# Two-layer diffusion backbone on one core: layer norms that work in PSUM, high-part products first, MLP blocks three ahead

## The chip, the core and the metric

The kernel runs on one core of one Trainium2 chip. The metric is the time of one execution in microseconds (us) of device time, as the median of several runs. Five engines matter here: TensorE (PE in the profile, PEld for its weight loads), VectorE (DVE), ScalarE (ACT), GpSimd (POOL) and SyncE (SP), which issues most DMAs.

## What is computed

384 tokens (128 context, 256 latent; three tiles of 128) pass through two layers. The part of a layer around the change, from the reference:

```python
y, extra = mixer_fn(x * (1 + sc1) + sh1)
x = _layernorm(ALPHA * x + g1 * y, lp['ln1_g'], lp['ln1_b'])
h = x * (1 + sc2) + sh2
f = jnp.square(jax.nn.relu(h @ lp['w_up'])) @ lp['w_down']
x = _layernorm(ALPHA * x + g2 * f, lp['ln2_g'], lp['ln2_b'])
```

`mixer_fn` ends in a product with `w_o` (1024 x 1024). The MLP is 1024 to 4096 to 1024. The layer's output, modulated by the next layer's shift and scale, goes into the next input projection, whose first chunk has 416 columns.

## The kernel before

**Arithmetic.** Every float32 product is three float32r products of high and low parts (`mm3`, lines 119 to 122): high by high, then the two mixed ones. A part is made by a cast (ACT, line 281 for weights, 1207 for activations) and a subtraction (DVE, `split_low`, line 125). Weights come through a ring of four split tiles.

**PSUM.** There are eight banks of 512 columns: psa 3, pso 1, psg 2, psm 2. A product with `w_o` or `w_down` accumulates 3 token tiles x 2 halves of 512 columns in the six banks of psa, pso and psg; psm holds transposes and the MLP's up blocks.

**`out_product` (line 1233)** runs `w_o` (8 weight rows of 128) and `w_down` (32). All but the last four rows go over all six banks. The last four (REST) are then done token tile by token tile (`last_part`), so that the norm of tile 0 runs beside the matmuls of tile 1. From there to the end of the function everything is recorded under `in_order`: each compute engine keeps the order in which the code is written. I call this stretch a tail. There are four: after `w_o` and after the MLP in each layer, at about 370, 645, 1006 and 1281 us.

**A tail, per tile (`layer_norm`, line 1152).** `raw` takes a half from its bank (DVE: gate times bank into z, line 1164; plus ALPHA x, line 1165; statistics, line 1167). `stats` ends the mean and variance (DVE lines 1170 to 1173, POOL's power at line 188, POOL line 1174). `normalise` scales z (ACT line 1182; DVE line 1179 for the second half of tile 2). `turn` transposes z into two psm banks (PE line 1193), modulates from the bank into an SBUF tile `hx` in eight 128-column pieces (ACT line 1199; DVE line 1202 for the second half of tile 2) and casts both halves to the high part hTh (line 1207). `low` subtracts for hTl (line 125). `update` makes the new x on POOL (lines 1215, 1216).

**The product behind a norm** is `first_up` (384 columns of `w_up`, the MLP blocks 0 to 2, token-major) behind `w_o`, and `first_chunk` (416 columns) behind the first layer's MLP. Both use `mm3` for one row of weights after another, so the third matmul already needs hTl:

```python
following(0, 0, 1)
turn[1]()
low[1]()
following(0, 1, KT)
normalise[2]()
following(1, 0, 2)
turn[2]()
```

After `first_up`, `square_u` and `turn_u` (lines 1336 to 1350) square the blocks and transpose them back.

**The MLP** (`step_mlp`, line 1394) records the up block k + AHEAD and then the down product of block k; AHEAD is 2. Block f needs three of the eleven T1 buffers (r, uh, ul). Here a scheduler, not `in_order`, sets the engines' order.

**The last tail** has no product behind it. DVE ends the second half of tile 1 and both halves of tile 2 by itself (`end`, lines 1225 and 1227), POOL ends the rest, and the result is stored in halves (line 1418).

Of the kernel before, what the change touches and what calls it, by code (L numbers as in the profile page):

```python
# [9 lines left out]
F32 = mybir.dt.float32  # L10
# [6 lines left out]
P = 128  # L17
# [17 lines left out]
AHEAD = 2  # L35
# [58 lines left out]
def kernel(ctx, tc, a):  # L94
# [360 lines left out]
    for l in range(L):  # L455
# [696 lines left out]
        def layer_norm(t, banks, xt, consts, mod, final):  # L1152

            cnd = 0 if t == 0 else 1
            gb, lg_, lb_ = consts[cnd], consts[2], consts[3]
            st = p2.tile([P, 2, 6], F32, tag="lnst", name=nm("lnst"), bufs=2)
# [4 lines left out]
            lows = []  # L1161

            def raw(h):
                nc.vector.tensor_tensor(out=z[h], in0=banks[h], in1=gb[:, halves[h]], op=ALU.mult)  # L1164
                nc.vector.scalar_tensor_tensor(out=z[h], in0=xt[:, halves[h]], scalar=ALPHA, in1=z[h], op0=ALU.mult,  # L1165
                                               op1=ALU.add)
                nc.vector.bn_stats(st[:, h], z[h])  # L1167

            def stats():
                nc.vector.bn_aggr(mv, st)  # L1170
                nc.vector.tensor_scalar(out=rs[:, 0:1], in0=mv[:, 1:2], scalar1=EPS, scalar2=None, op0=ALU.add)  # L1171
                rsqrt(rs[:, 1:2], rs[:, 0:1], 1)
                nc.vector.tensor_scalar(out=rs[:, 2:3], in0=mv[:, 0:1], scalar1=-1.0, scalar2=None, op0=ALU.mult)  # L1173
                nc.gpsimd.tensor_tensor(out=rs[:, 3:4], in0=rs[:, 2:3], in1=rs[:, 1:2], op=ALU.mult)

            def normalise(n=2):
                for h in range(n):
                    if t == 2 and h == 1:
                        nc.vector.tensor_scalar(out=z[h], in0=z[h], scalar1=mv[:, 0:1], scalar2=rs[:, 1:2],
                                                op0=ALU.subtract, op1=ALU.mult)  # L1180
                    else:
                        nc.scalar.activation(z[h], z[h], AF.Identity, bias=rs[:, 3:4], scale=rs[:, 1:2])

            def turn():
                ms, mb = mod
                hxs = []
                lows.clear()
                for h in range(2):
                    tb = bank(psm)
                    hx = v2("hx")  # L1190
                    hxs.append(hx)
                    for i in range(4):
                        nc.tensor.transpose(tb[:, i * P:(i + 1) * P], z[h][:, i * P:(i + 1) * P], ident)
                    for i in range(4):
                        k = 4 * h + i
                        o = hx[:, i * P:(i + 1) * P]
                        src = tb[:, i * P:(i + 1) * P]
                        if t < 2 or h == 0:
                            nc.scalar.activation(o, src, AF.Identity, bias=mb[:, k, cnd:cnd + 1],
                                                 scale=ms[:, k, cnd:cnd + 1])  # L1200
                        else:
                            nc.vector.tensor_scalar(out=o, in0=src, scalar1=ms[:, k, cnd:cnd + 1],
                                                    scalar2=mb[:, k, cnd:cnd + 1], op0=ALU.mult, op1=ALU.add)
                for h in range(2):
                    hv = hxs[h].rearrange("p (k n) -> p k n", k=4)
                    dh, dl = (q[:, 4 * h:4 * h + 4, t * P:(t + 1) * P] for q in hT)
                    nc.scalar.copy(dh, hv)
                    lows.append((dl, hv, dh))

            def low():  # L1210
                for q in lows:
                    split_low(*q)

            def update(h):
                nc.gpsimd.tensor_tensor(out=xt[:, halves[h]], in0=z[h], in1=lg_[:, halves[h]], op=ALU.mult)
                nc.gpsimd.tensor_tensor(out=xt[:, halves[h]], in0=xt[:, halves[h]], in1=lb_[:, halves[h]], op=ALU.add)
# [5 lines left out]
            def end(n):  # L1222

                for h in range(2 - n, 2):
                    nc.vector.scalar_tensor_tensor(out=z[h], in0=z[h], scalar=mv[:, 0:1], in1=lg_[:, halves[h]],  # L1225
                                                   op0=ALU.subtract, op1=ALU.mult)
                    nc.vector.scalar_tensor_tensor(out=xt[:, halves[h]], in0=z[h], scalar=rs[:, 1:2],  # L1227
                                                   in1=lb_[:, halves[h]], op0=ALU.mult, op1=ALU.add)
                    final(t, xt, halves[h])

            return raw, stats, normalise, turn, low, update, end

        def out_product(n_k, lhs, rhs, norm, rest, following, step=None, between=lambda i: None):
# [17 lines left out]
            raw, stats, normalise, turn, low, update, end = zip(*lns)  # L1251

            def last_part(t, within=None):
                steps = [(h, i) for h in range(2) for i in range(rest)]
# [5 lines left out]
                for n, (h, i) in enumerate(steps):  # L1260
                    if within and n == 2:
                        within()
                    w, x = tail[i]
                    mm3(banks[2 * t + h], tuple(q[:, t * P:(t + 1) * P] for q in x),
                        tuple(q[:, h * 512:(h + 1) * 512] for q in w), False, i == rest - 1)
                for h in range(2):
                    raw[t](h)
                    if within and h == 0:
                        low[t - 2]()
                stats[t]()  # L1270

            with in_order():
                last_part(0)
                normalise[0]()
                update[0](0)
                last_part(1)
                if following is None:
                    update[0](1)
                    end[1](1)
                    normalise[1](1)  # L1280
                    update[1](0)
                    last_part(2)
                    end[2](2)
                    return
                update[0](1)
                last_part(2, turn[0])
                normalise[1]()
                following(0, 0, 1)
# [6 lines left out]
                low[2]()  # L1295
                update[1](0)
                update[1](1)
                following(1, 2, KT)
                update[2](0)
                update[2](1)  # L1300
                between(0)
                following(2, 0, 3)
                stream.ahead(1)
                between(1)
                following(2, 3, KT)
                between(2)
                stream.ahead()
                between(3)
# [44 lines left out]
        def first_evac(i):  # L1353
            if i == 0:
                square_u(0)
            elif i == 1:
                square_u(1)
                turn_u(0)
            elif i == 2:
                turn_u(1)  # L1360
            else:
                square_u(2)
                turn_u(2)
# [3 lines left out]
        def first_up(t, k0, k1):  # L1367
            if k0 == 0:
                u_banks.append(bank(psa))
            proj_part(u_banks[t], w_u0, U0 * P, t, k0, k1)  # L1370
# [23 lines left out]
        def step_mlp(k):  # L1394
# [27 lines left out]
        def first_chunk(t, k0, k1):  # L1422
            if k0 == 0:
                banks_a.append(bank(psa))
            proj_part(banks_a[t], w_next, A_W, t, k0, k1)
# [163 lines left out]
```

## Time and profile before

| | us |
|---|---|
| median of 3 runs | 1311.73 |
| lowest, highest | 1308.55, 1313.06 |
| the profiled execution | 1311.86 |
| its span, first to last instruction | 1310.1 |
| PE busy in the span | 1273.6 (97%) |
| DVE, ACT, POOL busy | 882.9, 572.7, 207.2 |
| mean granted TensorE clock | 0.993 |

The profile comes from one execution; 1.8 us of that execution lie outside its span. PE's matmuls are pipelined: a row's duration is longer than the distance to the next one's start, so a loss is read from starts, or from the idle time that a row names in brackets together with what ended it.

### The profile page before, as it was taken

To read this page: it belongs to the slowest core of one execution; us is meant where nothing else is said; L and a number is where in the kernel's file an instruction comes from. 1 tells how busy PE (TensorE), PEld (TensorE's weight loads), DVE (VectorE), ACT (ScalarE), POOL (GpSimd) and SP (SyncE) were. 2 spreads that over 40 slices of the span, in tenths; PEclk is the share of its full clock that TensorE was granted. 3 is DMA by queue.
4 is the path that set the end of the run, shared out by engine and by line. 5 is a ranking of instruction groups with operands and counts; after the bars stand their busy time and mean duration, and the time that the engine had idled before them with its cause. 6 is when DMAs were issued, how large, how long until landed. Compare 5 with 4: busy or idle time off the path is not lost. (4 is left out here: it accounts for less than half of the span.)

```text
span 1310.1 us, 19402 instructions
## 1 busy us (share of the span) xinstructions
PE 1273.6 (97%) x7350; PEld 1143.7 (87%) x7350; DVE 882.9 (67%) x1603; ACT 572.7 (44%) x1054; POOL 207.2 (16%) x218
## 2 busy tenths in 40 slices
PE   8899999999999999999999999999999899999996
PEld 5789888999987999999988988899998799999995
DVE  4555899996669999543484689967455893333336
ACT  4454345323534444454365545423343644444441
POOL 0010301323223000000071120012320600000003
PEclk9999999999999999999999999999999999999998
DMA  9832354666534888554313224553644263335321
GB/s 368 295 109 91 103 173 158 210 217 222 163 112 163 274 272 271 177 171 140 113 72 121 86 93 161 182 173 118 227 159 153 72 225 129 129 129 183 133 71 49
DMA packets 64686, 211.68 MB, mean 162 GB/s; under 512 B 9233, under 2 KB 13265, under 8 KB 64465
## 3 DMA queue, kind: packets, MB, share of 16 engines
q1 hardware_dynamic: 61872, 201.49, 45.6%
q0 software_dynamic: 2432, 8.42, 1.9%
q8 instruction: 58, 0.95, 0.3%
q10 hardware_dynamic: 288, 0.52, 0.1%
q14 instruction: 36, 0.29, 0.1%
HBM read 206.28 MB, written 4.13 MB: 161 GB/s over the span
## 5 line engine op out<-in xcount | busy, mean ns | idle before, releaser
L125 DVE TENSOR_TENSOR wl<-raw,wh 128x1024 fp32r<-128x1024 f32 x250 | 317.5, 1274 | 284.9 <-ACT wh L281 281.2
L281 ACT CAST wh<-raw 128x1024 fp32r<-128x1024 f32 x250 | 261.7, 1050 | 453.3 <-PE bank L121 300.0
L120 PE MATMUL bank<-hTh,wh 128*128 128x384 f32 x976 | 330.8, 339 | 0.0
L122 PE MATMUL bank<-hTh,wl 128*128 128x384 f32 x976 | 328.1, 336 | 0.0
L121 PE MATMUL bank<-hTl,wh 128*128 128x384 f32 x976 | 328.0, 336 | 0.0
L120 PEld LDWEIGHTS bank<-hTh,wh 128*128 128x128 f32 x976 | 183.8, 188 | 6.7 <-issue 2.2
L121 PEld LDWEIGHTS bank<-hTl,wh 128*128 128x128 f32 x976 | 183.7, 188 | 2.4 <-issue 0.3
L122 PEld LDWEIGHTS bank<-hTh,wl 128*128 128x128 f32 x976 | 183.7, 188 | 0.6 <-issue 0.3
L121 PE MATMUL bank<-wl,uh 128*128 128x512 f32 x384 | 150.4, 392 | 0.0
L122 PE MATMUL bank<-wh,ul 128*128 128x512 f32 x384 | 150.2, 392 | 0.0
L120 PE MATMUL bank<-wh,uh 128*128 128x512 f32 x384 | 149.4, 391 | 0.0
L370 DVE CUSTOM_DVE_ANT_0 acc<-raw,csr,bT 128x1024 bf16<-128x1024 f32 x80 | 103.7, 1319 | 0.0
L120 PE MATMUL bank<-wh,hTh 128*128 128x256 f32 x336 | 100.6, 299 | 2.8 <-ACT tmc L594 2.8
L1107 POOL TENSOR_TENSOR tt<-tt,tt 128x384 f32<-128x384 f32 x48 | 61.6, 1304 | 242.3 <-DVE tt L1106 235.7
L370 DVE CUSTOM_DVE_ANT_0 acc<-lnc,csr,bT 128x1024 bf16<-128x1024 f32 x80 | 99.6, 1278 | 0.0
L121 PE MATMUL bank<-wl,hTh 128*128 128x256 f32 x336 | 96.0, 286 | 0.0
L122 PE MATMUL bank<-wh,hTl 128*128 128x256 f32 x336 | 95.9, 285 | 0.0
L120 PEld LDWEIGHTS bank<-wh,uh 128*128 128x128 f32 x384 | 72.0, 188 | 15.4 <-ACT wh L281 0.8
L122 PEld LDWEIGHTS bank<-wh,ul 128*128 128x128 f32 x384 | 72.0, 188 | 15.0
L121 PEld LDWEIGHTS bank<-wl,uh 128*128 128x128 f32 x384 | 72.1, 188 | 13.8
L120 PEld LDWEIGHTS bank<-wh,hTh 128*128 128x128 f32 x336 | 64.7, 193 | 6.8 <-ACT tmc L594 3.1
L121 PEld LDWEIGHTS bank<-wl,hTh 128*128 128x128 f32 x336 | 64.8, 193 | 2.5 <-issue 1.6
(260 smaller groups left out, 1862.3 us busy)
## 6 DMA issues: line engine op xcount, KB each, us to landing
raw<-in_w_g_dram SPq DMA_DIRECT2D x64, 512.0 KB, 3.6
raw<-in_w_d_dram SPq DMA_DIRECT2D x64, 512.0 KB, 3.5
raw<-in_w_u_dram SPq DMA_DIRECT2D x58, 512.0 KB, 3.7
raw<-in_w_av_dram SPq DMA_DIRECT2D x40, 512.0 KB, 3.4
lnc<-in_w_av_dram SPq DMA_DIRECT2D x40, 512.0 KB, 4.4
raw<-in_w_q_dram SPq DMA_DIRECT2D x28, 512.0 KB, 4.5
raw<-in_w_ada_dram SPq DMA_DIRECT2D x16, 512.0 KB, 8.5
raw<-in_w_b_dram SPq DMA_DIRECT2D x16, 512.0 KB, 3.6
```

The lines of the kernel that those rows point to most:

```text
L120: mm(out, lhsT=a_hl[0], rhs=b_hl[0], start=start, stop=False)
L121: mm(out, lhsT=a_hl[0], rhs=b_hl[1], start=False, stop=False)
L122: mm(out, lhsT=a_hl[1], rhs=b_hl[0], start=False, stop=stop)
L125: nc.vector.tensor_tensor(out=low, in0=x, in1=high.bitcast(F32), op=ALU.subtract)
L281: nc.scalar.copy(wh, raw)
L370: nc.vector.tensor_tensor_reduce(out=alloc().bitcast(BF16), in0=w, in1=csr[:, c], scale=1.0, scalar=bT[:, l, u, b:b + 1], op0=ALU.mult, op ...
L1107: nc.gpsimd.tensor_tensor(out=acc[c], in0=acc[c], in1=t_, op=ALU.add)
```

## The change

- `raw` multiplies in the bank in place and reads it from there for the sum. In the first three tails z is still an SBUF tile; in the last one everything stays in the banks.
- `turn` modulates in the psm bank in place, for all three tiles the first half on ACT and the second on DVE; the tile `hx` is gone. The cast (`high`) and the subtraction (`low`) read the bank.
- `proj_high` does both products of hTh first (16 matmuls), `proj_low` the eight of hTl last.
- The order within a tail is rewritten: transposes of tile 0 after one step of tile 2's matmuls rather than two, POOL's update of tile 0 after the statistics of tile 1.
- AHEAD is 3, and the third transposition of the squared blocks moves behind the first up block.
- The last tail computes the last half of tile 2 in two pieces of 256 columns; tile 1 is ended by ACT and POOL, with one last addition on DVE.

```diff
-AHEAD = 2
+AHEAD = 3
+        def proj_high(b, w, n, t, k0, k1):
+            for k in range(k0, k1):
+                for i in range(2):
+                    mm(b[:, :n], lhsT=hcol(k, t)[0], rhs=w[k][i], start=k == 0 and i == 0, stop=False)
+        def proj_low(b, w, n, t):
+            for k in range(KT):
+                mm(b[:, :n], lhsT=hcol(k, t)[1], rhs=w[k][0], start=False, stop=k == KT - 1)
...
+            src = banks if mod is None else z
...
-                nc.vector.tensor_tensor(out=z[h], in0=banks[h], in1=gb[:, halves[h]], op=ALU.mult)
-                nc.vector.scalar_tensor_tensor(out=z[h], in0=xt[:, halves[h]], scalar=ALPHA, in1=z[h], op0=ALU.mult,
-                                               op1=ALU.add)
-                nc.vector.bn_stats(st[:, h], z[h])
+                nc.vector.tensor_tensor(out=banks[h][:, c], in0=banks[h][:, c], in1=gb[:, c0:c1], op=ALU.mult)
+                nc.vector.scalar_tensor_tensor(out=src[h][:, c], in0=xt[:, c0:c1], scalar=ALPHA, in1=banks[h][:, c],
+                                               op0=ALU.mult, op1=ALU.add)
+                for i in range(c.start, c.stop, width):
+                    nc.vector.bn_stats(st[:, len(groups)], src[h][:, i:i + width])
...
-                        o = hx[:, i * P:(i + 1) * P]
-                        src = tb[:, i * P:(i + 1) * P]
-                        if t < 2 or h == 0:
-                            nc.scalar.activation(o, src, AF.Identity, bias=mb[:, k, cnd:cnd + 1],
+                        o = tb[:, i * P:(i + 1) * P]
+                        if h == 0:
+                            nc.scalar.activation(o, o, AF.Identity, bias=mb[:, k, cnd:cnd + 1],
...
+                            nc.vector.tensor_scalar(out=o, in0=o, scalar1=ms[:, k, cnd:cnd + 1],
...
+                def first_turn():
+                    turn[0]()
+                    high[0](0)
+                    normalise[1]()
+                    high[0](1)
+                    update[0](0)
+                    update[0](1)
+                last_part(2, first_turn)
+                sums(2, lambda: (low[0](0), low[0](1)))
+                following(0, 0, 4)
                 turn[1]()
-                low[1]()
-                following(0, 1, KT)
+                high[1](0)
                 normalise[2]()
-                following(1, 0, 2)
+                high[1](1)
+                low[1](0)
+                low[1](1)
+                following(0, 4, KT)
+                following(0)
+                following(1, 0, 4)
                 turn[2]()
...
+                    normalise[1]()
+                    update[1](0, 0)
+                    cuts = (0, 512, 768, 1024)
+                    last_part(2, None, cuts)
+                    sums(2, None, cuts)
+                    for h in range(2):
+                        for part in range(2):
+                            end[2](h, part)
+                    update[1](1, 0)
+                    update[1](0, 1)
+                    update[1](1, 1, nc.vector)
...
+            if k == 0:
+                with held(last_issued()):
+                    turn_u(2)
```

How this moves instructions, at three places. First DVE in the first layer's `w_o` tail, from the second half of tile 2 (z_4037, bank_3886) to tile 2's first low part. hTl is the low part, hx_4180 and hx_4190 are the modulated halves of tile 1. Before:

```order
L1164 TENSOR_TENSOR z_4037<-bank_3886,lnc_3857 128x512
L1165 SCALAR_TENSOR_TENSOR z_4037<-x_3873,z_4037 128x512
L1167 BN_STATS lnst_4033<-z_4037 128x6
L1170 BN_AGGR lnmv_4034<-lnst_4033 128x2
L1171 TENSOR_SCALAR lnrs_4035<-lnmv_4034 128x1
L1173 TENSOR_SCALAR lnrs_4035<-lnmv_4034 128x1
L125 TENSOR_TENSOR hTl<-hx_4180,hTh 128x4x128
L125 TENSOR_TENSOR hTl<-hx_4190,hTh 128x4x128
L1179 TENSOR_SCALAR z_4037<-z_4037,lnmv_4034,lnrs_4035 128x512
L1202 TENSOR_SCALAR hx_4244<-bank_4243,ms_3863,mb_3865 128x128 x4
L125 TENSOR_TENSOR hTl<-hx_4234,hTh 128x4x128
```

And now, where bank_4182 and bank_4191 hold tile 1's modulated halves:

```order
L1178 TENSOR_TENSOR bank_3886<-bank_3886,lnc_3857 128x512
L1179 SCALAR_TENSOR_TENSOR z_4037<-x_3873,bank_3886 128x512
L1182 BN_STATS lnst_4033<-z_4037 128x6
L1186 BN_AGGR lnmv_4034<-lnst_4033 128x2
L1187 TENSOR_SCALAR lnrs_4035<-lnmv_4034 128x1
L1191 TENSOR_SCALAR lnrs_4035<-lnmv_4034 128x1
L1216 TENSOR_SCALAR bank_4191<-bank_4191,ms_3863,mb_3865 128x128 x4
L1197 TENSOR_SCALAR z_4037<-z_4037,lnmv_4034,lnrs_4035 128x512
L125 TENSOR_TENSOR hTl<-bank_4182,hTh 128x4x128
L125 TENSOR_TENSOR hTl<-bank_4191,hTh 128x4x128
L1216 TENSOR_SCALAR bank_4240<-bank_4240,ms_3863,mb_3865 128x128 x4
L125 TENSOR_TENSOR hTl<-bank_4231,hTh 128x4x128
```

The low parts of tile 1 moved behind the scaling of tile 2's second half, four modulations were added ahead of it, and the operands named hx became banks.

Second PE at the same tail, around the transposes of tile 2 (ident, z_4036 and z_4037), with the product of tile 1 in bank_4226 before and bank_4222 now (o_ tiles are the parts of `w_up`). Before:

```order
L121 MATMUL bank_4226<-o_3914,hTh 128x384
L122 MATMUL bank_4226<-o_3913,hTl 128x384
L1193 MATMUL bank_4233<-ident,z_4036 128x128 x4
L1193 MATMUL bank_4243<-ident,z_4037 128x128 x4
L120 MATMUL bank_4226<-o_3937,hTh 128x384
L121 MATMUL bank_4226<-o_3938,hTh 128x384
L122 MATMUL bank_4226<-o_3937,hTl 128x384
```

And now:

```order
L607 MATMUL bank_4222<-o_3937,hTh 128x384
L607 MATMUL bank_4222<-o_3938,hTh 128x384
L1208 MATMUL bank_4231<-ident,z_4036 128x128 x4
L1208 MATMUL bank_4240<-ident,z_4037 128x128 x4
L607 MATMUL bank_4222<-o_3973,hTh 128x384
L607 MATMUL bank_4222<-o_3974,hTh 128x384
```

No product of hTl stands ahead of the transposes any more; the eight of them follow at the end of the tile's product.

Third POOL in the last tail, from the power of tile 1 (lnrs_12402 before, lnrs_12384 now; x_10058 and x_10046 are tile 0, x_10060 and x_10048 tile 1). Before:

```order
L188 TENSOR_TENSOR lnrs_12402<-lnrs_12402,nhalf 128x1
L1174 TENSOR_TENSOR lnrs_12402<-lnrs_12402 128x1
L1215 TENSOR_TENSOR x_10058<-z_12399,lnc_12245 128x512
L1216 TENSOR_TENSOR x_10058<-x_10058,lnc_12247 128x512
L1215 TENSOR_TENSOR x_10060<-z_12403,lnc_12245 128x512
L1216 TENSOR_TENSOR x_10060<-x_10060,lnc_12247 128x512
L188 TENSOR_TENSOR lnrs_12407<-lnrs_12407,nhalf 128x1
```

And now:

```order
L188 TENSOR_TENSOR lnrs_12384<-lnrs_12384,nhalf 128x1
L1192 TENSOR_TENSOR lnrs_12384<-lnrs_12384 128x1
L1233 TENSOR_TENSOR x_10046<-z_12380,lnc_12265 128x512
L1236 TENSOR_TENSOR x_10046<-x_10046,lnc_12267 128x512
L1233 TENSOR_TENSOR x_10048<-z_12385,lnc_12265 128x512
L188 TENSOR_TENSOR lnrs_12389<-lnrs_12389,nhalf 128x1
L1233 TENSOR_TENSOR x_10048<-z_12386,lnc_12265 128x512
L1236 TENSOR_TENSOR x_10048<-x_10048,lnc_12267 128x512
```

Two POOL passes over tile 1 now follow the power of tile 2, which stood last before.

## Rows read from the trace of the kernel before

**Rows 1.** The page: busy time of each engine over the span.
```profile
PE 1273.6 (97%) x7350; PEld 1143.7 (87%) x7350; DVE 882.9 (67%) x1603; ACT 572.7 (44%) x1054; POOL 207.2 (16%) x218
```
**Rows 2.** Waits of PE: total us, times, longest us, over the whole span.
```profile
PE bank L1193 <- DVE z L1179: 5.0, 3, 1.7
PE bank L122 <- DVE hTl L125: 3.9, 5, 1.0
...
PE bank L1345 <- DVE r L1339: 1.7, 2, 0.8
```
**Rows 3.** Timeline of PE, layer 0 `w_o` tail: start, us, operation, idle before.
```profile
382.60 1.03 PE L1193 MATMUL bank<-ident,z 128*128 128x128 f32 x8
...
387.58 0.33 PE L120 MATMUL bank<-o,hTh 128*128 128x384 f32 x1
387.75 0.34 PE L121 MATMUL bank<-o,hTh 128*128 128x384 f32 x1
389.08 0.45 PE L122 MATMUL bank<-o,hTl 128*128 128x384 f32 x1 [0.98 <-DVE hTl L125]
...
394.87 0.44 PE L122 MATMUL bank<-o,hTl 128*128 128x384 f32 x1 [0.47 <-DVE hTl L125]
...
397.96 0.66 PE L1193 MATMUL bank<-ident,z 128*128 128x128 f32 x4 [1.69 <-DVE z L1179]
```
**Rows 4.** Timeline of DVE, the same tail.
```profile
391.72 0.21 DVE L1170 BATCH_NORM_AGGREGATE lnmv<-lnst 128x2 f32<-128x12 f32 x1
...
393.51 2.99 DVE L125 TENSOR_TENSOR hTl<-hx,hTh 128x512 fp32r<-128x512 f32 x2 [1.33 <-ACT hTh L1207]
396.43 1.48 DVE L1179 TENSOR_SCALAR z<-z,lnmv,lnrs 128x512 f32<-128x512 f32 x1
398.73 1.37 DVE L1202 TENSOR_SCALAR hx<-bank,ms,mb 128x128 f32<-128x128 f32 x4 [0.82 <-PE bank L1193]
```
**Rows 5.** Timeline of POOL, the same tail.
```profile
394.35 1.61 POOL L1216 TENSOR_TENSOR x<-x,lnc 128x512 f32<-128x512 f32 x1
395.92 1.71 POOL L1215 TENSOR_TENSOR x<-z,lnc 128x512 f32<-128x512 f32 x1
```
**Rows 6.** Timeline of ACT, the same tail: z of tile 0.
```profile
380.73 1.52 ACT L1182 ACTIVATE z<-z,lnrs 128x512 f32<-128x512 f32 x2 [9.12 <-POOL lnrs L1174]
```
**Rows 7.** Single lines 1164 and 1165: duration ns min/median/max, first and last start.
```profile
L1164 DVE TENSOR_TENSOR z<-bank,lnc x24: 673/686/692, 374.6 to 1300.2; 128x512 f32<-128x512 f32 x24
L1165 DVE SCALAR_TENSOR_TENSOR z<-x,z x24: 691/693/1544, 375.4 to 1300.9; 128x512 f32<-128x512 f32 x24
```
**Rows 8.** Groups by line and form: busy us, mean ns, idle before.
```profile
L125 DVE TENSOR_TENSOR o<-bank,o 128x384 fp32r<-128x384 f32 x12 | 6.6, 552 | 4.0 <-ACT o L681 3.8
L633 DVE TENSOR_TENSOR bank<-bank,cst 128x128 f32<-128x128 f32 x16 | 4.5, 291 | 1.5 <-PE bank L626 1.5
L125 DVE TENSOR_TENSOR hTl<-hx,hTh 128x384 fp32r<-128x384 f32 x8 | 4.4, 555 | 1.7 <-ACT hTh L496 1.7
L125 DVE TENSOR_TENSOR ul<-bank,uh 128x128 fp32r<-128x128 f32 x18 | 4.1, 280 | 1.8 <-ACT uh L1348 1.8
L949 DVE TENSOR_TENSOR atts<-bank,dtab 128x256 f32<-128x256 f32 x16 | 6.0, 413 | 0.0
...
L1199 ACT ACTIVATE hx<-bank,mb,ms 128x128 f32<-128x128 f32 x60 | 21.9, 466 | 12.3 <-PE bank L1193 12.3
```
**Rows 9.** Timeline of the last tail: PE, DVE and POOL.
```profile
1295.88 0.74 DVE L1225 SCALAR_TENSOR_TENSOR z<-z,lnmv,lnc 128x512 f32<-128x512 f32 x1
1297.56 0.39 PE L122 MATMUL bank<-wh,ul 128*128 128x512 f32 x1
1297.77 0.68 DVE L1164 TENSOR_TENSOR z<-bank,lnc 128x512 f32<-128x512 f32 x1
1303.65 1.05 POOL L188 TENSOR_TENSOR lnrs<-lnrs,nhalf 128x1 f32<-128x1 f32 x1
1306.21 0.75 DVE L1227 SCALAR_TENSOR_TENSOR x<-z,lnrs,lnc 128x512 f32<-128x512 f32 x1
```

More of the change, by code (lines that the diff above doesn't have):

```diff
@@ L1195, in turn, with parts, high, low @@
                         k = 4 * h + i
-                        o = hx[:, i * P:(i + 1) * P]
-                        src = tb[:, i * P:(i + 1) * P]
-                        if t < 2 or h == 0:
-                            nc.scalar.activation(o, src, AF.Identity, bias=mb[:, k, cnd:cnd + 1],
+                        o = tb[:, i * P:(i + 1) * P]
+                        if h == 0:
+                            nc.scalar.activation(o, o, AF.Identity, bias=mb[:, k, cnd:cnd + 1],
                                                  scale=ms[:, k, cnd:cnd + 1])
                         else:
-                            nc.vector.tensor_scalar(out=o, in0=src, scalar1=ms[:, k, cnd:cnd + 1],
+                            nc.vector.tensor_scalar(out=o, in0=o, scalar1=ms[:, k, cnd:cnd + 1],
                                                     scalar2=mb[:, k, cnd:cnd + 1], op0=ALU.mult, op1=ALU.add)
[L1204 to L1216, printed above, removed]
+            def parts(h):
+                return [q[:, 4 * h:4 * h + 4, t * P:(t + 1) * P] for q in hT], \
+                    turned[h].rearrange("p (k n) -> p k n", k=4)
+            def high(h):
+                (dh, _), hv = parts(h)
+                nc.scalar.copy(dh, hv)
+            def low(h):
+                (dh, dl), hv = parts(h)
+                split_low(dl, hv, dh)
+            def update(h, part=None, add=None):
+                if part != 1:
+                    nc.gpsimd.tensor_tensor(out=xt[:, halves[h]], in0=z[h], in1=lg_[:, halves[h]], op=ALU.mult)
+                if part == 0:
+                    return
+                (add or nc.gpsimd).tensor_tensor(out=xt[:, halves[h]], in0=xt[:, halves[h]], in1=lb_[:, halves[h]],
+                                                 op=ALU.add)
                 if mod is None:
@@ L1220, in update, with end @@
                     final(t, xt, slice(0, D))
[L1222 to L1227, printed above, removed]
+            def end(h, part):
+                if part == 0:
+                    nc.vector.scalar_tensor_tensor(out=banks[h], in0=banks[h], scalar=mv[:, 0:1],
+                                                   in1=lg_[:, halves[h]], op0=ALU.subtract, op1=ALU.mult)
+                else:
+                    nc.vector.scalar_tensor_tensor(out=xt[:, halves[h]], in0=banks[h], scalar=rs[:, 1:2],
                                                    in1=lb_[:, halves[h]], op0=ALU.mult, op1=ALU.add)
                     final(t, xt, halves[h])
-            return raw, stats, normalise, turn, low, update, end
+            return raw, stats, normalise, turn, high, low, update, end
         def out_product(n_k, lhs, rhs, norm, rest, following, step=None, between=lambda i: None):
@@ L1250, in out_product, with last_part @@
             lns = [norm(t, banks[2 * t:2 * t + 2]) for t in range(3)]
-            raw, stats, normalise, turn, low, update, end = zip(*lns)
-            def last_part(t, within=None):
-                steps = [(h, i) for h in range(2) for i in range(rest)]
+            raw, stats, normalise, turn, high, low, update, end = zip(*lns)
+            def last_part(t, within=None, cuts=(0, 512, 1024)):
+                steps = [(c, e, i) for c, e in zip(cuts, cuts[1:]) for i in range(rest)]
                 if t == 0:
@@ L1259, in last_part, with sums @@
                         steps.insert(rest, steps.pop(rest + 1))
-                for n, (h, i) in enumerate(steps):
-                    if within and n == 2:
+                for n, (c, e, i) in enumerate(steps):
+                    if within and n == 1:
                         within()
                     w, x = tail[i]
[L1264 to L1269, printed above, removed]
+                    h = c // 512
+                    mm3(banks[2 * t + h][:, c - 512 * h:e - 512 * h], tuple(q[:, t * P:(t + 1) * P] for q in x),
+                        tuple(q[:, c:e] for q in w), False, i == rest - 1 and e % 512 == 0)
+            def sums(t, mid=None, cuts=(0, 512, 1024)):
+                for c, e in zip(cuts, cuts[1:]):
+                    raw[t](c, e)
+                    if mid and c == 0:
+                        mid()
                 stats[t]()
```

83 lines of the change are left out of this document (44 added, 39 removed).

## The prediction

> **What bounds the kernel now.** I read the page's busy times first: PE is busy 1273.6 of 1310.1 us, and no other engine passes 67% [rows 1]. So a change can help only where PE stands still, or after its last matmul. The waits of PE come next: lines 1193, 122 and 1345 wait for DVE's z, hTl and r, 10.6 us together [rows 2], all in the tails. The timelines of PE, DVE and POOL then show what each wait is made of in one tail, layer 0's `w_o`; layer 1's has the same program. Last I read the end of the span, where only DVE, POOL and ACT work.
>
> In that tail PE idles 0.98 for tile 0's hTl, 0.47 for tile 1's, 1.69 for tile 2's z [rows 3] and 0.8 for r (half of the 1.7 of line 1345) [rows 2]. Refilling the pipe adds to each: from 387.75 to 389.08 the starts are 1.33 apart where 387.58 to 387.75 shows 0.17, a loss of 1.16 for an idle of 0.98 [rows 3]. With 0.18 for each of four waits the tail loses 3.94 + 0.72 = 4.7. The tail behind layer 0's MLP has only a hTl and a z wait: 3.9 - 2 x 1.45 = 1.0 and 5.0 - 2 x 1.69 = 1.6 [rows 2, 3], 3.0 with the refills.
>
> DVE is late because POOL holds it. A pair of hTl takes 2.99, from 393.51 to 396.5, while POOL's line 1216 runs to 395.96; z then takes 1.48 and ends at 397.91, just behind POOL's 397.63 [rows 4, 5]. Line 1165, with two SBUF inputs, takes 691 ns mostly, but up to 1544; line 1164, with one operand in a bank, stays at 673 to 692 over all 24, spread over the same tails [rows 7]. I read from this that an operand in PSUM frees a DVE instruction of two inputs from POOL.
>
> **The change part by part.**
>
> *Working in the bank.* Lines 1179 and 125 get a PSUM operand. The instruction itself should cost the same: a subtraction of 128x384 takes 552 ns with a bank operand and 555 without [rows 8]. [...] Writing the bank too is shown by line 633, 291 ns at 128x128, against 280 for a subtraction of that shape into SBUF [rows 8]: 0.01 each, nothing over four. For ACT writing a bank there is no row; its modulation takes 466 ns into SBUF [rows 8]. I bound the difference at nothing and at a gain or loss of a tenth (0.05 each, 0.2 for a half) and take nothing, as DVE's rows show.
>
> *DVE's new order.* Tile 2's statistics end at about 391.5 in the layer-0 tail: the aggregation stood at 391.72 [rows 4] and the tail ended 0.4 later, a held line 1165 had cost up to 0.85 [rows 7], and tile 0's two low parts, 0.7 each (691 ns for that size [rows 7]), now stand ahead and take most of it back. Then four modulations of tile 1 at 1.37 / 4 [rows 4], to 392.9. Then z of tile 2, a scaling with one SBUF input, which POOL still holds: 1.1 to 1.5 (1.48 before [rows 4]), to 394.2. Then tile 1's low parts, now free of POOL: to 394.9 and 395.6.
>
> *PE's new order.* Tile 0's transposes move three matmuls earlier, from 382.60 to 381.9, but ACT's z ends at 380.73 + 1.52 = 382.25 [rows 3, 6]: a wait of 0.3. Behind tile 2's last matmul come 8 high products of tile 0 at 0.17, 8 transposes, 8 high and 8 low products, and 8 high products of tile 1: hTl is now wanted 3 us later, and the waits of 0.98 and 0.47 vanish. PE reaches tile 2's transposes at about 394.1. **A new wait** stands there: they need the two psm banks, which tile 1's modulated values hold until its low parts are read, at 394.9 and 395.6. I price it at 1.1, between 0.7 and 1.6. Queued behind it on PE are the other products of tile 1; ACT and DVE wait for its transposes. z itself, at 394.2, is hidden by it. The r wait shrinks to 0.4 since more of PE's products lie ahead of it, and the third turning, moved behind an up block, finds a bank of psm still read: 0.3. Sum of the new losses 0.3 + 1.1 + 0.4 + 0.3 = 2.1; gain 4.7 - 2.1 = 2.6 (1.5 to 3.5). Two tails: 5.2. In the MLP's tail only the new wait is left, with the same matmul times: 3.0 - 1.0 = 2.0 (1.0 to 2.5).
>
> *The last tail.* DVE got to tile 2 only at 1297.77, since ending tile 1 from 1295.88 kept it [rows 9]. That work goes to ACT and POOL; tile 2's first half (three instructions of 0.69) is over before PE ends. PE's last matmul starts at 1297.56 [rows 9]; twelve more matmuls in narrower pieces put its end at about 1298.1. The two 256-column pieces lie in one bank, and DVE's first piece waits for the bank's last matmul, so only the chain gets shorter, not the overlap. [...] From 1298.1: six instructions of 0.44 (413 ns for 128x256 [rows 8], and a little issue) to 1300.75; aggregation and epsilon 0.4; POOL's power some 0.6 instead of the 1.05 [rows 9] it had beside line 1225, to 1301.8; two halves of two passes at 0.75 [rows 9], the first already running, to 1304.1; then a last addition that waits for POOL, to 1305.1. Before, that was 1306.21 + 0.75 = 1306.96 [rows 9]. Gain 1.9, between 1.0 and 2.5.
>
> *AHEAD 3.* It takes three more T1 buffers out of eleven early; no wait of PE for uh or ul stands in its list, and r's two are those of the turnings [rows 2]. Price nothing; between a gain of 0.5 and a loss of 2.
>
> **Sum.** 5.2 + 2.0 + 1.9 = 9.1, against the profiled execution's 1311.86 (span 1310.1 and 1.8 around it): 1302.8. The median of the runs is 1311.73, so the same holds for it within 0.2.
>
> **Rivals.**
> - *Working in banks does not free DVE from POOL.* Then banks are held until the late low parts. Line 1179 takes 0.85 more twice, and the pair of low parts 2.99 rather than 1.4, ahead of the psm banks: 2 x 0.85 + 2 x 1.6 = 4.9 more in each `w_o` tail and, with one pair, 3.7 in the MLP's. 1302.8 + 9.8 + 3.7 = 1316.3, **slower**. It decides from about 1 us for one low part beside POOL. Against it: 24 of 24 of line 1164 [rows 7]. Chance 0.05.
> - *The psm wait eats half.* If z is held by a whole pass of POOL and tile 2's statistics come late, the transposes wait 2.5 instead of 1.1: 1.4 more in three tails, 4.2, which gives 1307.0. For it: DVE is the engine of all these waits. Chance 0.17.
> - *All waits vanish.* Then 2 x 4.7 + 3.0 + 2.5 go but for the first 0.3 three times, 14.0: 1297.9. Against it: the program makes PE wait for the low parts. Chance 0.1.
> - *AHEAD 3 leaves no free T1 buffer* and PE waits once in each block, 0.1 or more over some 60 blocks: 6 or more, 1308.8 and up. Chance 0.03.
> - *The pieces don't do what they say*: this is in the forecast already; if they did overlap, some 0.5 less.
>
> **How the numbers follow.** The forecast has 0.65. Its own bounds: tails 3.0 to 7.0, MLP 1.0 to 2.5, end 1.0 to 2.5, so 1299.9 to 1306.9. The range, 1298.5 to 1308.0, adds the rival of half the gain and part of the one without waits. A measurement can tell about 0.3%, 3.9 us, from no change. Faster by more: the forecast, the third rival and most of the half gain, 0.78. Within: the rest of it and the forecast's unknowns, 0.16. Slower: the first rival and a part of AHEAD's, 0.06.
>
> **What would show it.** Line 122's wait for hTl and z's wait of 1.7 gone; the transposes of line 1208 waiting about 1 us for hTl of line 125 instead; lines 1179 and 125 at 0.70 beside POOL while 1197 is still held; POOL's power in the last tail near 0.6; DVE's last instruction some 7 us behind PE's last matmul, not 9. Low parts above 1 us, new waits of PE inside the MLP, or the transposes waiting over 2 us would make it wrong.

## The result, and the profile after

The changed kernel takes 1299.05 us in the median of 4 runs (1297.76 to 1301.76), the kernel before 1312.39 in runs on the same chip; the ratio is 0.9902, 95% interval 0.9882 to 0.9922. That is faster by 13.3 us; 1302.8 was forecast.

The page of the changed kernel (busy us, share of the span, instructions), against [rows 1]:

```profile
span 1296.2 us, 19421 instructions
PE 1269.4 (98%) x7362; PEld 1142.7 (88%) x7362; DVE 877.9 (68%) x1629; ACT 566.9 (44%) x1031; POOL 199.0 (15%) x218
```

Its waits of PE (total us, times, longest), of the tails alone, against [rows 2]:

```profile
PE bank L1395 <- DVE r L1389: 2.3, 4, 0.7
...
PE bank L1208 <- DVE hTl L125: 0.9, 2, 0.5
```

The waits for z and for hTl in the products are gone, 8.9 us in all. In their place the transposes of tile 2 wait for psm banks, and r is waited for four times instead of twice.

PE in layer 0's `w_o` tail (start, us, operation, idle before), against [rows 3]:

```profile
387.84 1.55 PE L611 MATMUL bank<-o,hTl 128*128 128x384 f32 x8
389.23 1.55 PE L607 MATMUL bank<-o,hTh 128*128 128x384 f32 x8
391.23 1.16 PE L1208 MATMUL bank<-ident,z 128*128 128x128 f32 x8 [0.45 <-DVE hTl L125]
...
397.31 0.55 PE L1395 MATMUL bank<-ident,r 128*128 128x128 f32 x3 [0.72 <-DVE r L1389]
...
401.09 0.55 PE L1395 MATMUL bank<-ident,r 128*128 128x128 f32 x3 [0.45 <-DVE r L1389]
```

DVE in the same tail, against [rows 4]:

```profile
388.03 1.78 DVE L1216 TENSOR_SCALAR bank<-bank,ms,mb 128x128 f32<-128x128 f32 x4
389.72 0.77 DVE L1197 TENSOR_SCALAR z<-z,lnmv,lnrs 128x512 f32<-128x512 f32 x1
390.41 1.28 DVE L125 TENSOR_TENSOR hTl<-bank,hTh 128x512 fp32r<-128x512 f32 x2
392.44 1.78 DVE L1216 TENSOR_SCALAR bank<-bank,ms,mb 128x128 f32<-128x128 f32 x4 [0.75 <-PE bank L1208]
394.37 1.29 DVE L125 TENSOR_TENSOR hTl<-bank,hTh 128x512 fp32r<-128x512 f32 x2 [0.15 <-ACT hTh L1225]
395.58 1.68 DVE L1389 TENSOR_TENSOR r<-r 128x384 f32<-128x384 f32 x1
```

POOL in the same tail, against [rows 5]:

```profile
388.91 1.30 POOL L1233 TENSOR_TENSOR x<-z,lnc 128x512 f32<-128x512 f32 x1
390.28 1.34 POOL L1236 TENSOR_TENSOR x<-x,lnc 128x512 f32<-128x512 f32 x1
```

Tile 1's low parts take 1.28 for the pair while POOL's second pass runs beside them; the pair took 2.99 before. Still stretched are the square of r, with both inputs in SBUF (1.68, where the shortest of its six takes 0.54), and by some 0.2 the scaling of z (0.77; what it takes alone is shown at combo4).

**Where the time went, by stretches.** I cut PE's timeline at first matmuls that both programs have. Those of the changed kernel are these, and the last matmul:

```profile
384.15 0.33 PE L607 MATMUL bank<-o,hTh 128*128 128x384 f32 x1
...
656.34 0.35 PE L607 MATMUL bank<-o,hTh 128*128 128x416 f32 x1
...
678.01 0.49 PE L760 MATMUL bank<-wmla,sq 128*128 128x384 f32 x1
...
1013.90 0.33 PE L607 MATMUL bank<-o,hTh 128*128 128x384 f32 x1
...
1285.09 0.28 PE L122 MATMUL bank<-wh,ul 128*128 128x256 f32 x1
```

The same five in the kernel before: 387.58 and 1297.56 stand in [rows 3, 9]; the other three are

```profile
662.84 0.35 PE L120 MATMUL bank<-o,hTh 128*128 128x416 f32 x1
...
687.62 0.49 PE L750 MATMUL bank<-wmla,sq 128*128 128x384 f32 x1
...
1023.52 0.33 PE L120 MATMUL bank<-o,hTh 128*128 128x384 f32 x1
```

Their differences make seven stretches: **S0** up to the first product behind `w_o`; **S1** from there to the first behind the MLP (it holds the rest of the first tail); **S2** to the first matmul on `wmla` in layer 1 (the MLP's tail); **S3** to the product behind `w_o` in layer 1, which the change does not touch; **S4** to the last matmul; **S5** to the end of DVE's last instruction; **S6** to the span's end.

| us | S0 | S1 | S2 | S3 | S4 | S5 | S6 | S1 to S6 |
|---|---|---|---|---|---|---|---|---|
| before | 387.58 | 275.26 | 24.78 | 335.90 | 274.04 | 9.40 | 3.14 | 922.52 |
| changed | 384.15 | 272.19 | 21.67 | 335.89 | 271.19 | 7.27 | 3.84 | 912.05 |
| gain | 3.43 | 3.07 | 3.11 | 0.01 | 2.85 | 2.13 | -0.70 | 10.47 |

S3 agrees to 0.01, so a stretch tells tenths where the median of a few runs tells microseconds. The change gains 10.5. The 3.4 of S0 had come about before the first altered instruction: DVE's first product with the gate starts at 374.64 before and at 371.20 with the change. They go with the granted clock of TensorE. This is the windows view of the kernel before for two stretches (us, busy by engine, granted clock, DMA share, GB/s):

```profile
50.00:60.00 10.00, 7.23 (x36) 6.56 (x35) 9.57 (x18) 8.02 (x14) 0.94 (x2) 0.83 0.68 227
310.00:320.00 10.00, 8.06 (x39) 7.76 (x39) 5.08 (x13) 1.81 (x3) 4.96 (x6) 0.83 0.78 269
```

and of the changed kernel:

```profile
50.00:60.00 10.00, 7.70 (x52) 7.01 (x51) 9.54 (x17) 8.94 (x19) 1.11 (x2) 1.00 0.61 193
310.00:320.00 10.00, 8.14 (x48) 7.85 (x47) 5.00 (x11) 3.25 (x5) 3.29 (x6) 1.00 0.84 301
```

In the first, TensorE's granted clock was 0.50 for a part of both stretches (from 56.7 to 59.1, and from 315.6 to 318.6, products of 128x384 starting 0.32 apart there instead of 0.17), each time behind an idle of PE (2.77 for line 594's copy, 1.94 for line 1009's); in the changed kernel it was not, behind idles of 2.30 and 1.86 in the same places. Over the fourteen profiles of this study S0 lies between 383.97 and 389.10: 384 in the two where both stretches show 1.00, 385.8 to 387.9 in the four where one is below, 387.2 to 389.1 in the eight where both are (combo5, at 0.84 and 1.00, has 385.83; before_banks, at 0.83 twice, 387.48). So 10.5 is what the change does, and the profile shown happens to be one without a drop. The interval of the ratio, 10.2 to 15.5 us, holds 10.5.

### The profile page after: what moved, and what is told of

Read it like the earlier page. It is cut to its first block, busy times and chain, and to the rows that moved or that the text cites. A ratio compares the mean times of both kernels' runs of the same rounds, so it can differ in the third digit from the quotient of the medians.

```text
span 1296.2 us, 19421 instructions
## 1 busy us (share of the span) xinstructions
PE 1269.4 (98%) x7362; PEld 1142.7 (88%) x7362; DVE 877.9 (68%) x1629; ACT 566.9 (44%) x1031; POOL 199.0 (15%) x218
## 5 line engine op out<-in xcount | busy, mean ns | idle before, releaser
L121 PE MATMUL bank<-wl,uh 128*128 128x512 f32 (+1 forms) x388 | 151.1, 389 | 0.0
L122 PE MATMUL bank<-wh,ul 128*128 128x512 f32 (+1 forms) x388 | 150.9, 390 | 0.0
L120 PE MATMUL bank<-wh,uh 128*128 128x512 f32 (+1 forms) x388 | 150.3, 387 | 0.0
```

The lines of the kernel that those rows point to most:

```text
L120: mm(out, lhsT=a_hl[0], rhs=b_hl[0], start=start, stop=False)
L121: mm(out, lhsT=a_hl[0], rhs=b_hl[1], start=False, stop=False)
L122: mm(out, lhsT=a_hl[1], rhs=b_hl[0], start=False, stop=stop)
```

## The experiments

**Theory A**: a DVE instruction with two SBUF inputs stands still while POOL works, one with an operand in PSUM does not; DVE's queue sets the tails, so the bank operands make most of the gain. **Theory B**: the new order of products and low parts makes it. Further questions: AHEAD 3, the pieces of the last tail, and what is late next. I read each from the stretches:

| us | S0 | S1 | S2 | S3 | S4 | S5 | S6 | S1 to S6 |
|---|---|---|---|---|---|---|---|---|
| changed | 384.15 | 272.19 | 21.67 | 335.89 | 271.19 | 7.27 | 3.84 | 912.05 |
| before_banks | 387.48 | 272.76 | 22.16 | 335.88 | 271.52 | 7.77 | 3.13 | 913.22 |
| sum_sbuf | 388.30 | 273.18 | 22.61 | 335.92 | 272.21 | 7.26 | 3.92 | 915.10 |
| hx_sbuf | 386.15 | 276.35 | 24.29 | 335.91 | 276.30 | 7.26 | 3.84 | 923.95 |
| mm3_order | 387.48 | 272.32 | 23.18 | 335.86 | 271.33 | 7.27 | 3.86 | 913.82 |
| ahead2 | 383.97 | 272.36 | 21.66 | 335.89 | 271.37 | 7.27 | 3.88 | 912.43 |
| cuts512 | 388.39 | 272.16 | 21.65 | 335.89 | 270.94 | 6.71 | 3.86 | 911.21 |
| end_pool | 386.33 | 272.16 | 21.65 | 335.89 | 271.19 | 6.60 | 3.98 | 911.47 |
| square_act | 387.92 | 270.31 | 21.67 | 335.89 | 269.27 | 7.27 | 3.87 | 908.28 |
| low_first | 388.54 | 272.31 | 22.44 | 335.87 | 271.35 | 7.26 | 3.93 | 913.16 |
| combo3 | 389.10 | 270.26 | 21.64 | 335.88 | 269.02 | 6.38 | 3.92 | 907.10 |
| combo4 | 387.21 | 270.31 | 21.72 | 335.87 | 269.02 | 6.38 | 3.99 | 907.29 |
| combo5 | 385.83 | 270.31 | 21.71 | 335.88 | 269.01 | 6.38 | 3.98 | 907.27 |

**sum_sbuf: the sum back in SBUF.**

```diff
-nc.vector.tensor_tensor(out=banks[h][:, c], in0=banks[h][:, c], in1=gb[:, c0:c1], op=ALU.mult)
-nc.vector.scalar_tensor_tensor(out=src[h][:, c], in0=xt[:, c0:c1], scalar=ALPHA, in1=banks[h][:, c],
+nc.vector.tensor_tensor(out=src[h][:, c], in0=banks[h][:, c], in1=gb[:, c0:c1], op=ALU.mult)
+nc.vector.scalar_tensor_tensor(out=src[h][:, c], in0=xt[:, c0:c1], scalar=ALPHA, in1=src[h][:, c],
...
```

> The product of gate and bank goes to the SBUF tile z again in the first three tails, so line 1179 has two SBUF inputs; all else is the change. Theory A (an operand in PSUM keeps DVE free of POOL): some of its 18 instructions take 1.0 to 1.5 us instead of 0.69, tile 2's statistics come 0.5 to 1.3 us later, the stretch from the first product behind w_o to the first behind the MLP grows from 272.2 by 0.5 to 1.3, the whole kernel by 1.5 to 4. Theory B (the new order alone gives the gain): 0.69 each, no change within 0.3 in any stretch.

S1, S2 and S4 each lost 0.9 to 1.0. Line 1179 (duration ns min/median/max), first here, then in the changed kernel:

```profile
L1179 DVE SCALAR_TENSOR_TENSOR z<-x,z x18: 691/692/1714, 376.1 to 1023.1; 128x512 f32<-128x512 f32 x18
```

```profile
L1179 DVE SCALAR_TENSOR_TENSOR z<-x,bank x18: 686/689/689, 371.9 to 1016.0; 128x512 f32<-128x512 f32 x18
```

Theory A, near the middle of its range.

**hx_sbuf: the modulation back into an SBUF tile.**

```diff
-turned.append(tb)
+hx = v2("hx")
+turned.append(hx)
...
-o = tb[:, i * P:(i + 1) * P]
+o = hx[:, i * P:(i + 1) * P]
+s = tb[:, i * P:(i + 1) * P]
...
-nc.scalar.activation(o, o, AF.Identity, bias=mb[:, k, cnd:cnd + 1],
+nc.scalar.activation(o, s, AF.Identity, bias=mb[:, k, cnd:cnd + 1],
...
-nc.vector.tensor_scalar(out=o, in0=o, scalar1=ms[:, k, cnd:cnd + 1],
+nc.vector.tensor_scalar(out=o, in0=s, scalar1=ms[:, k, cnd:cnd + 1],
...
```

> The modulation writes an SBUF tile again, and cast and low part read that; all else is the change. Theory A: low parts beside POOL go from 0.64 to 1.3 or more, and as the psm banks now come free with the modulation, the transposes of tile 2 wait for z, not for hTl: their wait changes from 0.45 to anything between 0 and 0.8, and waits for r grow because DVE is late, by 0.5 to 1.0 each; whole kernel +1 to +4. Theory B: the low parts stay at 0.64, the wait for the banks goes, -1 to -2.

Theory A in kind, and far above its range: +11.9 us by the stretches, so that the whole gain is gone (median 1313.06, ratio to before 1.0004, 0.9990 to 1.0017). The psm banks did come free earlier; it did not help. The low parts (ns min/median/max; 18 of the 26 are the tails') and the first of PE's waits:

```profile
L125 DVE TENSOR_TENSOR hTl<-hx,hTh x26: 550/1745/1784, 10.5 to 1036.1; 128x512 fp32r<-128x512 f32 x18, 128x384 fp32r<-128x384 f32 x8
```

```profile
PE bank L1397 <- DVE r L1391: 7.6, 2, 3.8
```

Fifteen of the 18 low parts in the tails take 1.74 to 1.78 instead of 0.68, r stands behind them in DVE's queue, and PE waits 3.8 for r in both `w_o` tails. I had put the growth of that wait at 0.5 to 1.0.

Not all of the 11.9 is the hold. Behind both waits of 3.8 TensorE's granted clock was lower for a while (0.83 and 0.66 over 10 us, behind the times of the five engines):

```profile
400.00:410.00 10.00, 7.06 (x34) 7.03 (x35) 8.52 (x13) 2.78 (x9) 3.94 (x3) 0.83 0.47 157
1036.00:1046.00 10.00, 6.52 (x25) 6.49 (x26) 7.89 (x10) 1.84 (x7) 4.47 (x3) 0.66 0.47 156
```

PE behind the first of the two waits, and in the same place of the changed kernel:

```profile
403.24 2.89 PE L607 MATMUL bank<-o,hTh 128*128 128x384 f32 x8
405.93 1.92 PE L611 MATMUL bank<-o,hTl 128*128 128x384 f32 x8
407.69 0.49 PE L1397 MATMUL bank<-ident,r 128*128 128x128 f32 x3
```

```profile
397.61 1.64 PE L607 MATMUL bank<-o,hTh 128*128 128x384 f32 x8
399.10 1.55 PE L611 MATMUL bank<-o,hTl 128*128 128x384 f32 x8
```

The sixteen products take 4.45 (403.24 to 407.69). In the changed kernel, at a granted clock of 1.00, eight high ones take 1.49 (397.61 to 399.10) and eight low ones 1.39 (387.84 to 389.23), 2.88 together. That is 1.6 lost in S1; in layer 1 the transposes and products of that place take 5.68 (1039.48 to 1045.16) against 0.30 + 2.88, 2.5 lost in S4. By this estimate 4.1 of the 11.9 are the clock's, which fell behind a wait that the hold had made, and 7.8 the hold's own, still about twice the upper end of my range.

**before_banks: the operands alone, in the kernel before.**

```diff
-nc.vector.tensor_tensor(out=z[h], in0=banks[h], in1=gb[:, halves[h]], op=ALU.mult)
-nc.vector.scalar_tensor_tensor(out=z[h], in0=xt[:, halves[h]], scalar=ALPHA, in1=z[h], op0=ALU.mult,
+nc.vector.tensor_tensor(out=banks[h], in0=banks[h], in1=gb[:, halves[h]], op=ALU.mult)
+nc.vector.scalar_tensor_tensor(out=z[h], in0=xt[:, halves[h]], scalar=ALPHA, in1=banks[h], op0=ALU.mult,
...
-hx = v2("hx")
+hx = tb
```

> The kernel before with the bank operands alone: the gated sum reads its second operand from the bank (also in the last tail), and the modulation stays in the psm bank, read there by cast and low part; order, products, AHEAD and last tail as before. Theory A (free operands make most of the gain): line 1165 at 0.69 in all 24, a pair of low parts at 1.3 to 1.4 instead of up to 2.99; the stretch from the first product behind w_o to the first behind the MLP falls from 275.3 by 1.5 to 2.5, the one over the MLP's tail from 24.8 by 1.0 to 2.5, DVE's end behind PE from 9.4 by about 1; 5.5 to 8 of the 10.4 us. Theory B (operands help only together with the order): under 3 us of them.

9.3 of the 10.5 us: 2.50, 2.62 and 2.52 in S1, S2 and S4 and 1.63 in S5, over the range I gave (median 1302.47, ratio to before 0.9927, 0.9909 to 0.9945). The sum's instructions take 686 to 689 in all 24, and in this kernel, with the old order of products and low parts, PE has no wait for hTl left in a tail, only two shorter ones for z:

```profile
PE bank L1193 <- DVE z L1179: 1.4, 2, 0.7
```

Theory B is out: everything else in the change adds 1.2 us on top. In the last tail it adds nothing: from the start of the last matmul to the end of the span the kernel before takes 12.54, this one 10.90 with the old order of that tail, and the change 11.11, with a last matmul that starts 0.25 later for its narrower pieces (cuts512).

**mm3_order: the products of hTl back in each row.**

```diff
-for i in range(2):
-    mm(b[:, :n], lhsT=hcol(k, t)[0], rhs=w[k][i], start=k == 0 and i == 0, stop=False)
+mm3(b[:, :n], hcol(k, t), w[k], k == 0, k == KT - 1)
...
-for k in range(KT):
-    mm(b[:, :n], lhsT=hcol(k, t)[1], rhs=w[k][0], start=False, stop=k == KT - 1)
+pass
```

> The three products of a weight row stand together again, so hTl is wanted with the first row; all else is the change. Theory A with the order as a second cause: tile 0's hTl is wanted at its tail's 384.5 and ready at 384.9, a wait of 0.3 to 0.6; tile 1's is wanted at 389.6 and ready at 391.1, a wait of 1.0 to 1.5, in place of the transposes' 0.45. Each tail +0.8 to +1.5, the kernel +2.4 to +4.5. If free operands alone make the gain: no wait over 0.2 for hTl, the kernel within 0.6.

S2 lost 1.51, but S1 and S4 only 0.13 and 0.14. The waits for hTl are back, two in each tail:

```profile
PE bank L122 <- DVE hTl L125: 2.5, 6, 0.5
```

In the first tail they are 0.35 and 0.50, the second well under the 1.0 to 1.5 that I had put there. Behind `w_o` PE then arrives late and r is ready, with no wait for it left in the list: the wait moves. High products first pay only behind the MLP, where no r follows.

**ahead2: AHEAD 2 again.**

```diff
-AHEAD = 3
+AHEAD = 2
```

> AHEAD is 2 again, the third turning stays in the first step of the MLP. Forecast's pricing (nothing): the stretches of the MLP stay within 0.4 us each. Rival (blocks three ahead give a part of the gain, since 3.1 us were gained in each stretch where 2.6 and 2.0 were forecast): +0.5 to +1.5 in each of the two stretches that hold an MLP.

0.17 and 0.18 more: the forecast's pricing holds.

**cuts512: the last half in one piece.**

```diff
-width = 256 if mod is None and t == 2 else 512
+width = 512
...
-cuts = (0, 512, 768, 1024)
+cuts = (0, 512, 1024)
```

> The last tail computes and sums the second half of tile 2 in one piece of 512 columns; all else is the change. Theory A (the pieces share a bank and so wait for its last matmul; six instructions of 0.46 stand where three of 0.70 would do): PE ends 0.26 earlier, DVE needs 2.1 instead of 2.9 behind it, the end comes 0.8 to 1.1 earlier. Theory B (the pieces shorten the end, as the change's words have it): the end comes 0.3 to 0.8 later.

S4 is 0.25 and S5 0.56 shorter, 0.8 together, as theory A has it. The changed kernel's DVE behind the last matmul:

```profile
1285.40 0.43 DVE L1178 TENSOR_TENSOR bank<-bank,lnc 128x256 f32<-128x256 f32 x1 [0.65 <-PE bank L122]
1285.94 0.43 DVE L1179 SCALAR_TENSOR_TENSOR bank<-x,bank 128x256 f32<-128x256 f32 x1
...
1287.81 0.43 DVE L1182 BATCH_NORM_STATS2 lnst<-bank 128x6 f32<-128x256 f32 x1
```

Its first piece starts only after the last matmul (1285.09), so cutting bought no overlap, and six instructions of 0.43 need 2.84 (1285.40 to 1288.24) where three of 0.70 need 2.24 in cuts512. The pieces of the change cost time.

**end_pool: POOL ends tile 1 alone, the first half ahead of its power.**

```diff
-update[1](0, 0)
+update[1](0)
...
-update[1](1, 0)
-update[1](0, 1)
-update[1](1, 1, nc.vector)
+update[1](1)
```

> POOL does both halves of tile 1 by itself, the first before its power of tile 2, in the time in which it now stands idle (1287.1 to 1288.8); DVE ends with tile 2; all else is the change. Theory A (the end is DVE's queue plus stores that pile up, 0.7 us more behind the last instruction than before the change): last instruction 0.4 to 0.6 earlier, stores spread, span 0.7 to 1.3 shorter. Theory B (the last store alone sets the 3.8 us): 0.4 to 0.6 shorter. If POOL's pass delays the power: longer by 0.5 or more.

DVE ends 0.67 earlier, the span 0.5 to 0.6: theory B's number, POOL's last pass now ending 0.24 behind DVE. That the stores pile up is seen all the same. GB/s of all DMA queues in 40 slices over the last 10 us, before the change and with it:

```profile
GB/s 0 0 0 0 0 0 336 377 393 385 385 221 0 0 0 0 0 156 393 377 123 0 0 0 0 106 369 393 180 0 0 213 393 393 49 0 0 0 0 0
```

```profile
GB/s 0 0 221 393 385 49 0 0 0 0 0 0 0 0 0 0 0 0 0 57 385 393 213 0 0 147 385 385 344 393 385 377 385 336 8 0 0 0 0 0
```

Before, the last store of 256 KB had the queues to itself; with the change three run back to back, and S6 grew by 0.70.

**square_act: r squared by ACT.**

```diff
-nc.vector.tensor_tensor(out=r, in0=r, in1=r, op=ALU.mult)
+nc.scalar.activation(r, r, AF.Square)
```

> The squares of the first three up blocks are taken by ACT (as in the MLP's other blocks) instead of DVE; all else is the change. Theory A (behind w_o DVE's chain, at its end a square with two SBUF inputs that POOL holds to 1.64 to 1.68, sets the end, and that is why another order of the products cost only 0.13 there): r's waits of 0.72 and 0.45 fall under 0.15, each w_o tail 1.1 to 1.5 shorter, the kernel 2.2 to 3.0. Theory B (the psm banks or the weights come late next): under 0.5 each.

1.88 and 1.92 in S1 and S4, above the range; PE's waits for r are gone from the list (the two of 0.72 and 0.45, and with them the pipe's refills). DVE's queue, with the last held instruction at its end, was what set the `w_o` tails of the changed kernel. The run takes the square out of the hold and out of DVE's queue at once; it does not tell the two apart.

**low_first: one low part ahead of the scaling of z.**

```diff
+low[1](0)
 normalise[2]()
 high[1](1)
-low[1](0)
 low[1](1)
```

> Tile 1's first low part stands ahead of the scaling of tile 2's second half on DVE, so the first psm bank comes free earlier; all else is the change. Theory A (the transposes wait for banks, but behind w_o r is the later wait): the wait of 0.45 falls under 0.2; 0.3 to 0.6 gained behind the MLP, 0 to 0.2 behind each w_o. Theory B (the bank wait sets the end of each of these tails): 0.3 to 0.6 gained in all three.

A miss for both: S2 is 0.77 longer, and the transposes wait up to 1.3 instead of 0.45. Behind `w_o` S1 and S4 lose only 0.12 and 0.16, since r's waits shrink from 2.3 in four to 0.9 in two. DVE and POOL of this kernel in the first tail:

```profile
394.10 0.68 DVE L125 TENSOR_TENSOR hTl<-bank,hTh 128x512 fp32r<-128x512 f32 x1
394.70 1.52 DVE L1197 TENSOR_SCALAR z<-z,lnmv,lnrs 128x512 f32<-128x512 f32 x1
```

```profile
394.67 1.27 POOL L1236 TENSOR_TENSOR x<-x,lnc 128x512 f32<-128x512 f32 x1
```

The scaling has one SBUF input and is held too: it ends at 396.22, 0.28 behind POOL's 395.94. In the changed kernel it ends at 390.49, again 0.28 behind POOL's 390.21, and before at 397.91 against 397.63 [rows 4, 5]. It starts 0.8 into POOL's pass in the changed kernel, and here with it: 0.77 against 1.52.

**combo3: square_act, cuts512 and end_pool together.** Its edits are those three.

> Three edits of the changed kernel together: squares on ACT, last tail in one piece of 512 columns, tile 1's end on POOL alone. If they are separate causes, they add: 1.9 + 1.9 + 0.8 + 0.5 = 5.1 us below the changed kernel; the two long stretches at 270.3 and 269.0, the span ending 9.8 us behind the start of the last matmul instead of 11.1. If they hide each other: under 3.

They add: 4.95 us below the changed kernel by the stretches, where the three alone make 5.2.

**combo4 and combo5, on top of combo3: the scaling of tile 2 reads its bank; then the low part ahead of it as well.**

```diff
-src = banks if mod is None else z
+src = banks if mod is None else [z[0], banks[1] if t == 2 else z[1]]
```

> The three edits, and the second half of tile 2's sum stays in its bank until DVE scales it, so that line 1197 reads a bank, too. Theory A: 1197 falls from 0.77 to 0.55 to 0.70 and is no longer held by POOL; each of three tails 0.1 to 0.2 shorter than with the three edits. If a scaling with one SBUF input is not held, no change.

> As the last one, and tile 1's first low part ahead of that scaling. The low part ahead cost 0.8 behind the MLP when the scaling read SBUF (held to 1.52). Theory A (the hold alone made that loss): with the bank as input the loss goes, the transposes' wait of 0.45 falls under 0.3, each of three tails 0.1 to 0.5 shorter than with three edits. Theory B (the second psm bank decides): the wait stays at 0.4 to 0.8.

Neither gains: S1, S2 and S4 stay within 0.08 of combo3's. The hold is gone, and the scaling of line 1197 is slow in another way. First combo5, then the kernel before_banks:

```profile
L1197 DVE TENSOR_SCALAR z<-bank,lnmv,lnrs x3: 802/802/806, 392.0 to 1019.9; 128x512 f32<-128x512 f32 x3
```

```profile
L1179 DVE TENSOR_SCALAR z<-z,lnmv,lnrs x3: 537/1585/1585, 394.5 to 1025.3; 128x512 f32<-128x512 f32 x3
```

The one of 537 in before_banks, behind the MLP, began just ahead of a POOL pass:

```profile
667.23 0.54 DVE L1179 TENSOR_SCALAR z<-z,lnmv,lnrs 128x512 f32<-128x512 f32 x1
```

```profile
667.35 1.56 POOL L1215 TENSOR_TENSOR x<-z,lnc 128x512 f32<-128x512 f32 x1
```

Here it was POOL that stood still: that pass takes 1.56, the two beside it in the trace 1.28 and 1.29. In the kernel before, line 1165 took 693 to 694 where it began 0.04 ahead of POOL's line 1174, and that line 0.71 instead of 0.20. So the hold works both ways: in these rows the engine that begins first runs through and the other ends late.

So 537 is the scaling unheld. The bank costs 0.27, about what the hold cost in the changed kernel. The low part ahead no longer loses 0.77, so the hold did make that loss; but the transposes still wait 0.6 at the longest, as the other theory had it.

Measured against before, combo3 has 0.9883 (0.9862 to 0.9903), combo4 0.9886 (0.9867 to 0.9905) and combo5 0.9879 (0.9861 to 0.9897, median 1295.90). The intervals overlap that of the change, 0.9882 to 0.9922; that these three kernels beat it is shown by the stretches, 4.8 to 4.95 us, not by the medians alone.

## Why the prediction was right, and where it was not

- **What bounds it** held: PE's waits in the tails and the end were all there was to win; S3 moved by 0.01.
- **POOL holds DVE** held, in both directions: 686 to 689 with the bank operand, up to 1714 without. The rival in which banks do not free DVE, 1316.3, is out. Held beside POOL in these runs were instructions with two SBUF inputs (low parts 1.74 to 1.78 against 0.68, the square 1.68 against 0.54) and the scaling from SBUF (1.52 against 0.54). What the forecast did not have is that POOL stands still just as well where DVE begins first (1.56 against 1.28, and 0.71 against 0.20). (The rival's 3.7 for the MLP's tail does not follow from its own prices: 2 x 0.85 + 1.6 is 3.3, which makes 1315.9; that changes nothing here.)
- **High products first make the hTl waits vanish** was true of the new order of DVE, where mm3_order has them back, 2.5 us in six. But it was not the reason for the gain: before_banks, with the old order of products and of low parts, has no such wait either, and mm3_order gives back only 0.13 and 0.14 in the `w_o` tails.
- **The `w_o` tails**: 2.6 each forecast, 3.07 and 2.85 measured (3.1 for the second, since S4 holds 0.25 of narrower matmuls, as cuts512 shows). The new wait at the transposes, 1.1 forecast, has 0.45 of idle: z's scaling took 0.77 rather than 1.1 to 1.5, since it met the end of a POOL pass. The r wait went the other way: 0.4 forecast, 0.72 and 0.45 found. The two waits of 0.3, at tile 0's transposes and at the third turning, did not come. With 0.18 of refill for each of the three waits found the new losses are 2.2, against 2.1 forecast; so the waits do not account for the 0.5 that the tail gained beyond the forecast, of which AHEAD 3 has 0.17. The rest stays open.
- **The MLP's tail**: 2.0 forecast, 3.11 measured, the largest miss. The new wait was carried over whole from the `w_o` tails, but line 1208's two waits are theirs; behind the MLP none is listed. Its products of 416 columns keep PE busy longer (eight low ones take 1.51 from start to start, 660.22 to 661.73 in the changed kernel, against 1.39 for 384 columns), which fits; no run tried that alone.
- **The last tail**: 1.9 forecast, for the work on tile 1 that moves off DVE. DVE's end came 2.13 - 0.25 = 1.9 earlier against PE's work, but 0.70 went to stores on each other's heels, which the forecast left at their old 3.14. The power at 0.55 and the pieces' lack of overlap were as forecast; that the pieces lose against one whole half I had not worked out. And the reason was mostly another: before_banks, which moves no work, has 1.63 of DVE's 2.13 and keeps the old 3.13 behind it.
- **AHEAD 3 at nothing** held (0.35 in all).
- **The sum**: 9.1 forecast, 10.5 by the stretches. The rest of the distance from 1302.8 to the profiled 1298.03 is S0's 3.4. The forecast took the profiled execution of before as a fixed start and named no spread of its own for the clock. The median, 1299.05, lies 0.55 above the lower end of the range, 1298.5; the change's own 10.5 off the profiled 1311.86 would be 1301.4. How close the median came to the end of the range was the clock's draw, not a finding on the mechanism.

## What to carry to other kernels

Where POOL and DVE work side by side, look for DVE instructions whose longest time is twice the shortest: giving one of their operands a place in PSUM was worth 9 of 10 us here, without a change of order. Cutting the last piece smaller cost 0.8 us here: with the two pieces in one bank, the consumer started only behind the producer's last instruction (1285.40 behind 1285.09). Compare two profiles by stretches between instructions that both have; a stretch that the change does not touch tells how fine the comparison is.

## What was not expected of the hardware

- A scaling of 128x512 takes 537 ns from SBUF (before_banks), 802 from a bank (combo5); why is not shown. The instructions with two tensor inputs lost nothing (691 against 689).
- Modulating in place is a little dearer on DVE, 1.78 for four pieces against 1.37 [rows 4], and cheaper on ACT, 431 ns against 466 [rows 8].
- The granted clock fell behind an idle of PE of 1.9 to 2.8 us at the same two places in most profiles and not in all of them, whatever the kernel (to 0.83 to 0.87 over 10 us in before, before_banks, combo3 and combo4, at both places); idles of 2.30 and 1.86 in the changed kernel and of 2.1 in combo5, in the same places, passed at 1.00. In hx_sbuf it also fell behind both idles of 3.8 (0.83 and 0.66). What decides it stays open.
